# Small matrix products that share the TensorE array: emitted one by one, or as one item per set

## The chip, the cores and the metric

The kernel runs on one NeuronCore of a Trainium2 chip. The metric is the device time of one execution in microseconds (us). The kernel before was timed three times on its own; the median is the number to compare with. All rows below come from one profiled execution of it.

## What is computed

Four transformer blocks on 256 tokens of width 1024, batch 1, in fp32. Each of the ten stages of these blocks is a norm with a shift and scale that come from a conditioning vector, then a mixer or a feed-forward layer, then a gate. Cut to what the change touches:

```python
mod = silu(c) @ ada_w[i] + ada_b[i]            # shift, scale, gate of every stage
h = rms_norm(x, ln) * (1.0 + scale) + shift
x = x + gate * mixer_or_ffn(h)

# mixers: diff_attention, spatial_gating, hgrn2_mixer, nsa_mixer. Of nsa_mixer, for each head:
s_s = q @ k_sel.T * scale - slope * dist        # selected branch
s_w = q @ k_win.T * scale - slope * dist        # window branch
s_c = q @ k_cmp.T * scale - slope * dist_c      # compressed branch, 15 blocks
o = gate0 * softmax(s_c) @ v_cmp + gate1 * softmax(s_s) @ v_sel + gate2 * softmax(s_w) @ v_win
```

At this length all blocks are selected, so the selected branch and the window branch see the same 256 positions, with keys and values of their own.

## The kernel before, in words

**A recorded program.** The methods of `Model` do not emit instructions. Each call on an engine is recorded by `Plan.add` as an `Op` with a priority (its place in the recording), its predecessors and a price from `Plan.price`. `Plan.order` then plays a list scheduler over the five engines: when an engine is free in its model, the ready op of the lowest number goes next, if its tiles find slots (`SLOTS`: 8 PSUM banks `ps`, 4 weight buffers `raw`, 6 `whi`, 6 `wlo`). `Plan.emit` emits all ops in that order (L480), so every instruction carries the line L486, and each engine runs its part strictly in the order planned. Tiles are therefore the way to find a place in the trace.

**The large products.** A weight block arrives by DMA in `raw`; ScalarE writes its high part `whi` and VectorE the remainder `wlo`; TensorE takes three products per pair of tiles (`hhi`·`whi`, `hlo`·`whi`, `hhi`·`wlo`). Up-projections write `pg`, `pv`, `pa`, `pq`, `pc` (256 columns each), down-projections `pd` and the first layer's `pgv` (512 columns).

**The small products.** These are plain fp32 matmuls, which the trace shows as two passes each, and they use part of the 128x128 array:
- `ada` in `first` (L956): shift and scale of the first stage. For each of eight tiles k of the model dimension, 2 x 4 matmuls, each 128 rows by 32 columns of the array, the four of a round in four column strips. Their sums pass through `adas` and `adac` to the columns that scale tile k; beside that the 12 `pgv` products of tile k-1 run. Each k loads 1 MiB of `ada_w` and 0.5 MiB of the feed-forward weights.
- `ada` in `mod_pe` (L706): the same for stage 9, eight sets of four matmuls of 512 columns, worked out beside stage 8.
- `modc` (`mod_cols`, L736) and `modg` (`mod_gate`, L759): sets of four in column strips, beside the feed-forward layers.
- `pl` in `attend` (L1204): logits of the differential attention. Four matmuls per half of the tokens, 64 rows each, two per row strip, recorded map by map.
- `pst` in `recur` (L1403): sets of 16 (or 8, 4) matmuls in column strips of 32 or 64, strip by strip within a block.
- In `nsa_group` (L1637), run for 4 groups of heads and t = 1, 0 (second and first half of the tokens): `npl`, the logits of one head on 64 rows, even heads on rows 0 to 63 and odd heads on rows 64 to 127, one bank each; and `no`, the output of the four heads. `no` has two accumulations in two column strips of 64 (even heads, odd heads), each of one product with the compressed values (`lcT`) and 2 (t = 0) or 4 (t = 1) with the others (`nT`). They are recorded one accumulation after the other:

```python
for e in range(2):
    pairs = [(vc[:, g], lct[0:15, e])]
    pairs += [(vs[br][:, k, es], pts[e][br][:, k]) for br in range(2) for k in range(t + 1)]
    self.mms(o[64 * e:64 * e + 64], pairs)
```

In the model of the kernel before, `price` (L262) gives a matmul of 33 to 64 output rows half of its full time and one of up to 32 a quarter, each by itself; an op of a higher priority number that is ready goes between two ops of such a set whenever the next one of the set is not yet allowed.

Of the kernel before, what the change touches and what calls it, by code (L numbers as in the profile page):

```python
# [54 lines left out]
class Tl:  # L55
    """A tile; those with a tag share the slots of that tag."""
# [57 lines left out]
class Vw:  # L114
    """A view of a tile: how to make it, and which elements it covers."""
# [76 lines left out]
# the scheduler's model: from the end of an instruction to the start of one that waits for it  # L192
# [13 lines left out]
class Plan:  # L206
    ENGINES = ("tensor", "scalar", "vector", "gpsimd", "sync")

    def __init__(self, nc, slots, reserve):
        self.nc, self.slots, self.reserve = nc, slots, reserve  # L210
        self.ops = []
        self.psum = None
        self.shift = 0
        self.turn = None
        self.regret = 2.0
        self.patience = 3000.0
        for e in self.ENGINES:
            setattr(self, e, PlanEngine(self, e))

    def add(self, eng, method, args, kw):  # L220
        op = Op()
        op.eng, op.method, op.args, op.kw = eng, method, args, kw
        op.prio = len(self.ops) + self.shift
        op.succ, op.npred, op.tiles = [], 0, []
# [5 lines left out]
        reads += pos  # L230
# [26 lines left out]
        op.cost, op.late = self.price(op, reads, writes)  # L257
# [4 lines left out]
    def price(self, op, reads, writes):  # L262
        """(what it holds its engine for, what comes on top until its results can be used), in the model"""
        n = max(int(np.prod(v.shape[1:])) for v in (writes[-1:] if op.eng == "tensor" else reads + writes) or reads)
        if op.eng == "sync":
            v = (writes + reads)[0]
            size = int(np.prod(v.shape)) * 4
            return 450.0, size / 360.0
        if op.eng == "tensor":
            if op.method == "transpose":  # L270
                return 109.0, 60.0
            n = int(np.prod(op.args[2].shape[1:]))
            if op.args[2].tl.dtype == F32R:
# [5 lines left out]
        if op.eng == "scalar":  # L279
            aps = sum(isinstance(op.kw.get(x), Vw) for x in ("scale", "bias", "accum_out"))  # L280
            return (51.0 if ps else 94.0) + n * 0.833 + 93.0 * aps, 40.0
        if op.eng == "gpsimd":
            if op.kw.get("op") == OP.pow:
# [3 lines left out]
        if op.method in ("tensor_scalar", "scalar_tensor_tensor"):  # L287
            aps = sum(isinstance(v, Vw) for v in op.args[2:4 if op.method == "tensor_scalar" else 3])
        if op.method in ("tensor_copy", "tensor_scalar", "memset") and not ps:
            return 67.0 + 0.52 * n + 60.0 * aps, 20.0  # L290
        if op.method == "reciprocal":
# [3 lines left out]
    def order(self):  # L295
# [34 lines left out]
        def fits(op):  # L330
            # engines take turns at a bank, for reads too
# [26 lines left out]
        while left:  # L358
            looks.clear()
            for e in self.ENGINES:  # L360
# [22 lines left out]
                if self.regret and e in ("scalar", "vector"):  # L383
                    # a more urgent one that is about to be ready goes first
# [95 lines left out]
    def emit(self):  # L480
# [3 lines left out]
        for op in self.order():  # L484
            f = getattr(getattr(self.nc, op.eng), op.method)
            f(*[real(v) for v in op.args], **{k: real(v) for k, v in op.kw.items()})  # L486
# [7 lines left out]
# the shift and scale (s) and the gate (g) of which stages are worked out beside which stage  # L494
# [6 lines left out]
# how many tiles of a layer's output product wait, to go by half of the tokens  # L501
# [4 lines left out]
class Model:  # L506
# [18 lines left out]
    def m(self, shape, name="m", dtype=F32):  # L525
        """Scratch of the mixers, in the space of the feed-forward activations."""
# [13 lines left out]
    def mms(self, out, pairs):  # L540
        """One accumulation group."""
# [20 lines left out]
    def load(self, t, src):  # L562
        """a weight load: it may run ahead, and the loads after it are issued after it"""
# [14 lines left out]
    def act_pair(self, a32, shape):  # L578
        """Exact high and low parts of an activation, as stationary operands."""
# [7 lines left out]
    def setup(self):  # L587
# [17 lines left out]
        # the first row of each quarter  # L605
# [5 lines left out]
    def columns(self, rows, name):  # L611
        """Vectors cut in rows of 128 -> one column per row."""
# [14 lines left out]
    def load_c(self):  # L627
        """silu of the conditioning vectors, each column 32 times"""
# [5 lines left out]
    def load_columns(self, names, name, maps=(), first=0):  # L634
        """vectors over the model dimension, eight columns each; with them the biases of the stages from `first` on"""
# [9 lines left out]
        if maps:  # L645
            # the 1 that goes with a scale is added here
# [6 lines left out]
    def stage(self, i):  # L653
        """weights, bias, first column, conditioning vector, norm and gate factor of a stage"""
# [25 lines left out]
    def mod_dve(self, i, key):  # L680
        """acc[p, n], with sum over p = (silu(c) @ w)[n] of shift, scale or gate (that with its bias); returns the steps"""
# [24 lines left out]
    def mod_pe(self, i):  # L706
        """shift and scale by matrix products: 512 columns in each quarter of the rows; returns the steps"""
# [3 lines left out]
        def step(k):  # L711
            def f():
# [4 lines left out]
                for j in range(4):  # L717
                    nc.tensor.matmul(self.accc[32 * j:32 * j + 32, :], self.csil[:, coff + k], t[:, j],
                                     start=k == 0, stop=k == 7)
# [8 lines left out]
    def mod_steps(self, item, pe):  # L728
        """Steps that gather the shift and scale, or the gate, of a stage."""
# [6 lines left out]
    def mod_cols(self, i, pe):  # L736
        """Shift and scale of a stage as columns."""
# [3 lines left out]
        else:  # L741
            s = self.pu([128, 512], "modc")
            for j in range(4):
                nc.tensor.matmul(s[32 * j:32 * j + 32, :], self.ones[:, 0:32],
                                 self.acc["sh" if j < 2 else "sc"][:, 512 * (j % 2):512 * (j % 2) + 512],
                                 start=True, stop=True)
# [12 lines left out]
    def mod_gate(self, i):  # L759
        nc = self.nc  # L760
        pt = self.pu([128, 256], "modg")
        for j in range(4):
            nc.tensor.matmul(pt[32 * j:32 * j + 32], self.ones[:, 0:32], self.acc["g"][:, 256 * j:256 * j + 256],
                             start=True, stop=True)
# [6 lines left out]
    def gate_load(self, i):  # L771
        """the gate of a stage, on all partitions"""
# [5 lines left out]
    def rstd(self, ss, parts):  # L778
        """(sum of the first `parts` columns + eps) ** -0.5"""
# [24 lines left out]
    def norm(self, h, r=None, xs=None, x=None):  # L804
        """rms norm with modulation, transposed, as exact high and low parts."""
# [30 lines left out]
    def norm_twice(self, h, row):  # L836
        """x <- rms norm of x times row; then the norm of the next layer."""
# [10 lines left out]
        # with a = mean square + eps: the two norms scale by a ** -.5 and (mean square of x times row / a + eps) ** -.5  # L848
# [13 lines left out]
    def up_t(self, w, c0, new, name):  # L862
        """h @ w[:, c0:c0+256], transposed: [column, 2, token]"""
# [35 lines left out]
    def down_mm(self, h, f, act, parts, cols=(0, 1)):  # L899
        """act = (high, low) parts [128, 256 tokens] of contraction tile f"""  # L900
# [46 lines left out]
    def flip_tokens(self, a):  # L947
        """[token, half, (2, 128)] -> PSUM [128, 2, (half, token)]"""
# [7 lines left out]
    def first(self, wg, wu):  # L956
        """The first norm, and the first 512 columns of the first layer along with it: both go by tiles of the
        model dimension, as the weights of shift and scale come in."""
# [35 lines left out]
        for k in range(9):  # L994
# [17 lines left out]
            for r in range(2):  # L1012
                for j in range(4):
                    nc.tensor.matmul(pa[32 * j:32 * j + 32], self.csil[:, coff + 2 * j + r], t[:, :, 2 * j + r],
                                     start=r == 0, stop=r == 1)
# [3 lines left out]
            for c in range(2):  # L1019
                nc.tensor.matmul(pc[:, c:c + 1], sums[:, c], self.sel, start=True, stop=True)  # L1020
# [95 lines left out]
    def seg_rstd(self, p, nseg, width, name):  # L1116
        """p: [128, nseg, width] -> rstd [128, nseg]"""
# [86 lines left out]
    def attend(self, hp, qt, kt, v):  # L1204
        nc = self.nc
        o_ps = self.pu([128, 2, 2, 128], "o")
        for t in range(2):
            n = 128 * (t + 1)
            # the two maps of both heads; a map's rows of the array write one bank
            lgs = []  # L1210
            sm = self.small(24, "smx")
            for c in range(2):
                cs = slice(64 * c, 64 * c + 64)
                pl = self.pu([128, 2, n], "pl")
                lg = self.m([128, 2, n], "lg")
                for h in range(2):
                    nc.tensor.matmul(pl[:, h], qt[cs, h, 128 * t:128 * t + 128], kt[cs, h, :n],
                                     start=True, stop=True)
# [29 lines left out]
    def to_act(self, on, g):  # L1248
        """[token, (head, half), 128] -> contraction tiles [128, head, token], scaled by column g"""
# [567 lines left out]
```

## Time and profile before

| | us |
|---|---|
| Median of 3 runs | 1757.2 |
| Lowest and highest run | 1753.75, 1757.4 |
| Span of the profiled execution, first to last instruction | 1755.1 |
| TensorE matmuls busy in that span | 1718.1 |
| VectorE busy | 1319.0 |
| ScalarE busy | 953.5 |
| GpSimd busy | 66.3 |

The profile records the span of its execution and not the device time around it; the span lies 2.1 us under the median of the runs, and that is taken as what lies around it. DMA moved 415.00 MB at a mean of 236 GB/s. In the trace a row of TensorE reads: start in us from the span's start, length of the piece in us, operation, output tile and inputs, rows x columns of the array, contraction rows x moving columns, and the number of records (two for each fp32 matmul). Lengths include the time that a result takes to leave the array; how long TensorE is held is the distance to the start of the next piece.

### The profile page before, as it was taken

The page shows a single profiled execution, that of the slowest core. Times are in us where ns is not written, and L with a number is a line of the kernel's source. Part 1 is how long each engine was busy: PE and PEld are TensorE (multiplying, and loading weights), DVE is VectorE, ACT ScalarE, POOL GpSimd, SP SyncE. Part 2 cuts the span into 40 slices and gives each one's busy share as a digit, 9 for nine tenths or more (in the row PEclk, how much of TensorE's full clock was granted, in tenths as well). Part 3 has the DMA queues.
Part 4 walks back from the last instruction along what each step waited for, and adds up shares of the span by engine and source line. Part 5 has one row for each costly group of instructions (what it writes and reads, how often), then busy time and mean ns, then how long its engine had stood idle before and what let it go on. Part 6 is the DMA issues. An engine that isn't in the chain of part 4 may idle for free. (4 is left out here: it accounts for less than half of the span.)

```text
span 1755.1 us, 31103 instructions
## 1 busy us (share of the span) xinstructions
PE 1718.1 (98%) x12678; PEld 1526.4 (87%) x12678; DVE 1319.0 (75%) x2045; ACT 953.5 (54%) x1595; POOL 66.3 (4%) x60
## 2 busy tenths in 40 slices
PE   7999999999999999999999999999999999999998
PEld 4899779899988999798999789979998876579986
DVE  3787679887777878687777788888985556678754
ACT  4454366664446544375444477866553556666542
POOL 0000012100001000000000000000000000000000
PEclk9999999999999999999999999999999999999999
DMA  9798866668886988574889863548887543247662
GB/s 299 266 333 316 284 213 225 206 219 284 294 297 220 344 297 326 180 267 168 294 274 326 328 193 104 199 145 277 290 300 264 191 145 129 82 145 239 201 221 72
DMA packets 264159, 415.00 MB, mean 236 GB/s; under 512 B 12890, under 2 KB 210373, under 8 KB 262993
## 3 DMA queue, kind: packets, MB, share of 16 engines
q1 hardware_dynamic: 264017, 413.03, 69.4%
q8 instruction: 99, 1.62, 0.4%
q14 instruction: 43, 0.35, 0.1%
HBM read 411.90 MB, written 1.10 MB: 235 GB/s over the span
## 5 line engine op out<-in xcount | busy, mean ns | idle before, releaser
L486 ACT ACTIVATE whi<-raw 128x1024 fp32r<-128x1024 f32 x512 | 534.2, 1056 | 516.7 <-PE pd L486 139.9
L486 DVE TENSOR_TENSOR wlo<-raw,whi 128x1024 fp32r<-128x1024 f32 x512 | 616.8, 1220 | 209.1 <-ACT whi L486 207.5
L486 PE MATMUL pv<-hhi,whi 128*128 128x256 f32 x912 | 257.4, 282 | 0.0
L486 PE MATMUL pv<-hhi,wlo 128*128 128x256 f32 x912 | 257.3, 282 | 0.0
L486 PE MATMUL pv<-hlo,whi 128*128 128x256 f32 x912 | 257.1, 282 | 0.0
L486 DVE SCALAR_TENSOR_TENSOR acc<-raw,csil,acc 128x1024 f32<-128x1024 f32 x192 | 245.9, 1281 | 14.4 <-DMA raw<-in_ada_w 11.7
L486 PE MATMUL pd<-whi,ahi 128*128 128x512 f32 x604 | 237.8, 395 | 0.0
L486 PE MATMUL pd<-wlo,ahi 128*128 128x512 f32 x604 | 237.7, 394 | 0.0
L486 PE MATMUL pd<-whi,alo 128*128 128x512 f32 x604 | 237.5, 394 | 0.0
L486 PE MATMUL pg<-hhi,whi 128*128 128x256 f32 x624 | 176.7, 283 | 0.0
L486 PE MATMUL pg<-hlo,whi 128*128 128x256 f32 x624 | 176.2, 282 | 0.0
L486 PE MATMUL pg<-hhi,wlo 128*128 128x256 f32 x624 | 176.0, 282 | 0.0
L486 PEld LDWEIGHTS pv<-hhi,whi 128*128 128x128 f32 x912 | 174.3, 191 | 1.2 <-issue 1.2
L486 PEld LDWEIGHTS pv<-hhi,wlo 128*128 128x128 f32 x912 | 174.4, 191 | 0.0
L486 PEld LDWEIGHTS pv<-hlo,whi 128*128 128x128 f32 x912 | 174.2, 191 | 0.0
L486 PEld LDWEIGHTS pd<-whi,ahi 128*128 128x128 f32 x604 | 113.4, 188 | 30.3 <-issue 5.8
L486 PEld LDWEIGHTS pd<-whi,alo 128*128 128x128 f32 x604 | 113.4, 188 | 25.6 <-issue 0.3
L486 PEld LDWEIGHTS pd<-wlo,ahi 128*128 128x128 f32 x604 | 113.5, 188 | 24.5
L486 PEld LDWEIGHTS pg<-hhi,whi 128*128 128x128 f32 x624 | 119.3, 191 | 2.5 <-issue 2.5
L486 PEld LDWEIGHTS pg<-hlo,whi 128*128 128x128 f32 x624 | 119.3, 191 | 0.1
L486 PEld LDWEIGHTS pg<-hhi,wlo 128*128 128x128 f32 x624 | 119.3, 191 | 0.0
L486 PE MATMUL pa<-hhi,whi 128*128 128x256 f32 x352 | 99.6, 283 | 0.0
(356 smaller groups left out, 3174.3 us busy)
## 6 DMA issues: line engine op xcount, KB each, us to landing
raw<-in_ada_w SPq DMA_DIRECT2D x112, 1024.0 KB
raw<-in_ffn_wd SPq DMA_DIRECT2D x44, 1024.0 KB
raw<-in_ffn_w_up SPq DMA_DIRECT2D x44, 1024.0 KB
raw<-in_ffn_wg SPq DMA_DIRECT2D x42, 1024.0 KB
raw<-in_ffn_wu SPq DMA_DIRECT2D x42, 1024.0 KB
raw<-in_ffn_w_down SPq DMA_DIRECT2D x22, 1024.0 KB
raw<-in_hg_w_in SPq DMA_DIRECT2D x16, 1024.0 KB
raw<-in_attn_w_qkv SPq DMA_DIRECT2D x12, 1024.0 KB
```

The source lines that it names most:

```text
L486: f(*[real(v) for v in op.args], **{k: real(v) for k, v in op.kw.items()})
```

## The change

A context manager `Plan.together` collects matmuls that are recorded inside it into one `Op`, a bundle. The bundle's predecessors are those of all its matmuls together, it becomes ready when all of them could go, holds the engine as one item and is emitted back to back. Its price is 95 ns plus the sum of its matmuls' prices, divided by `pairs`.

```diff
+    @contextmanager
+    def together(self, pairs=1):
+        assert self.bundle is None
+        self.bundle = calls = []
+        yield
+        self.bundle = None
+        self.add("tensor", "bundle", tuple(calls), {}, pairs)
...
+        if method == "bundle":
+            parts = [self.price(eng, m, a, k, *self.operands(a, k)) for m, a, k in args]
+            op.cost, op.late = 95.0 + sum(c for c, _ in parts) / pairs, 60.0
...
     def first(self, wg, wu):
...
+            with nc.together():
+                for r in range(2):
+                    for j in range(4):
+                        nc.tensor.matmul(pa[32 * j:32 * j + 32], self.csil[:, coff + 2 * j + r], t[:, :, 2 * j + r],
+                                         start=r == 0, stop=r == 1)
...
     def attend(self, hp, qt, kt, v):
...
+            with nc.together(2):
+                for h in range(2):
+                    for c in range(2):
...
     def nsa_group(self, g, t, q, vs, vc, gv):
...
+            if j % 2 == 0:
+                pls = [self.pu([128, 2, n], "npl") for e in range(2)]
+                with nc.together(2):
+                    for e in range(2):
+                        rs = slice(64 * e, 64 * e + 64)
+                        nc.tensor.matmul(pls[e], q[rs, j // 2, ts], kt[rs, :, :n], start=True, stop=True)
+            pl = pls[j % 2]
...
-        for e in range(2):
-            pairs = [(vc[:, g], lct[0:15, e])]
-            pairs += [(vs[br][:, k, es], pts[e][br][:, k]) for br in range(2) for k in range(t + 1)]
-            self.mms(o[64 * e:64 * e + 64], pairs)
+        with nc.together():
+            for i in range(len(terms[0])):
+                for e in range(2):
+                    nc.tensor.matmul(o[64 * e:64 * e + 64], *terms[e][i], start=i == 0, stop=i == len(terms[0]) - 1)
```

`mod_pe`, `mod_cols`, `mod_gate` and `recur` get a `together` around their sets as `first` does. In `attend` the rows of the two maps take turns; in `nsa_group` an even and an odd head share a bundle of `npl`, and the two strips of `no` take turns. The arithmetic is the same, instruction for instruction. The planner's other rules are as they were; since prices and sets differ, the order of all engines differs in places, ScalarE's 27 table loads keep their number.

On TensorE in `first`, around one k of the loop, the kernel before has:

```order
L486 MATMUL ada<-raw,csil 32x256 x5
L486 MATMUL pgv<-whi,hhi 128x512
L486 MATMUL ada<-raw,csil 32x256
L486 MATMUL pgv<-wlo,hhi 128x512
L486 MATMUL ada<-raw,csil 32x256
L486 MATMUL pgv<-whi,hlo 128x512
L486 MATMUL ada<-raw,csil 32x256
L486 MATMUL pgv<-whi,hhi 128x512
```

and the changed kernel:

```order
L511 MATMUL pgv<-whi,hlo 128x512
L511 MATMUL ada<-raw,csil 32x256 x8
L511 MATMUL pgv<-whi,hhi 128x512
L511 MATMUL pgv<-wlo,hhi 128x512
L511 MATMUL pgv<-whi,hlo 128x512
```

The last three of the eight `ada` stood alone between `pgv` products at four of the eight k (k = 2 to 5; the other four sets were whole already); now all eight sets are whole. In the same way `mod_pe`'s eight sets of four, four of which stood in two groups, are now whole. The sets `modc`, `modg` and all 28 small sets of `pst` stood back to back before, in the same order.

On TensorE in `nsa_group`, t = 0, around one `no` (buffer numbers kept; the two `nT` are those of even and of odd heads), the kernel before has:

```order
L486 MATMUL npl_16363<-kt_15146,q_15300 128x256
L486 MATMUL npT_16370<-ident_82,lg_16315 128x128
L486 MATMUL npl_16372<-kt_15146,q_15300 128x256
L486 MATMUL npT_16370<-ident_82,lg_16315 128x128
L486 MATMUL pd_16150<-whi_16022,nact_16074 128x512
L486 MATMUL no_16384<-lcT_16368,vc_15817 64x256
L486 MATMUL no_16384<-nT_16247,v_15038 64x256
L486 MATMUL no_16384<-nT_16247,v_15066 64x256
L486 MATMUL no_16384<-lcT_16368,vc_15817 64x256
L486 MATMUL no_16384<-nT_16291,v_15038 64x256
L486 MATMUL no_16384<-nT_16291,v_15066 64x256
```

and the changed kernel:

```order
L511 MATMUL npl_16371<-kt_15146,q_15301 128x256
L511 MATMUL npl_16373<-kt_15146,q_15301 128x256
L511 MATMUL pd_16085<-wlo_16087,nact_16064 128x512
L511 MATMUL no_16386<-lcT_16368,vc_15864 64x256 x2
L511 MATMUL no_16386<-nT_16284,v_15038 64x256
L511 MATMUL no_16386<-nT_16293,v_15038 64x256
L511 MATMUL no_16386<-nT_16284,v_15066 64x256
L511 MATMUL no_16386<-nT_16293,v_15066 64x256
L511 MATMUL npl_16406<-kt_15146,q_15301 128x256
L511 MATMUL npl_16408<-kt_15146,q_15301 128x256
```

Of the 32 `npl`, 20 stood alone (4 of t = 1, all 16 of t = 0); now all stand in pairs of an even and an odd head. The eight `no` sets stood whole, but strip after strip; now the strips take turns. The number of instructions on each engine is the same.

## Rows read from the trace of the kernel before

**Rows 1.** Page, busy us (share of the span) and instructions of each engine.
```profile
PE 1718.1 (98%) x12678; PEld 1526.4 (87%) x12678; DVE 1319.0 (75%) x2045; ACT 953.5 (54%) x1595; POOL 66.3 (4%) x60
```
**Rows 2.** Windows by stage: length, busy us by engine, granted clock, DMA share, GB/s.
```profile
0.00:60.00 60.00, 50.65 (x270) 30.22 (x271) 24.90 (x67) 24.89 (x51) 2.71 (x9) 1.00 1.01 296
...
1020.00:1160.00 140.00, 138.14 (x1795) 127.31 (x1795) 117.35 (x217) 114.27 (x231) 6.97 (x6) 1.00 0.48 155
...
1405.00:1488.00 83.00, 81.14 (x498) 58.90 (x496) 49.64 (x179) 48.52 (x118) 0.00 (x0) 0.94 0.41 141
1488.00:1550.00 62.00, 60.98 (x277) 34.96 (x277) 44.44 (x225) 38.31 (x136) 1.50 (x2) 1.00 0.19 63
```
**Rows 3.** Timeline of PE, the loop of `first`.
```profile
42.70 1.05 PE L486 MATMUL ada<-raw,csil 128*32 128x256 f32 x10
43.68 0.50 PE L486 MATMUL pgv<-whi,hhi 128*128 128x512 f32 x1
44.11 0.62 PE L486 MATMUL ada<-raw,csil 128*32 128x256 f32 x2
44.66 0.51 PE L486 MATMUL pgv<-wlo,hhi 128*128 128x512 f32 x1
...
46.96 0.40 PE L486 MATMUL pgv<-wlo,hhi 128*128 128x512 f32 x1
47.19 0.39 PE L486 MATMUL pgv<-whi,hlo 128*128 128x512 f32 x1
...
49.34 1.07 PE L486 MATMUL ada<-raw,csil 128*32 128x256 f32 x16
50.34 0.50 PE L486 MATMUL pgv<-whi,hhi 128*128 128x512 f32 x1
...
53.99 1.07 PE L486 MATMUL ada<-raw,csil 128*32 128x256 f32 x16
```
**Rows 4.** Timeline of PE, two `no` sets: t = 1, then t = 0.
```profile
1457.31 0.64 PE L486 MATMUL no<-lcT,vc 15*64 15x256 f32 x2
...
1459.75 0.64 PE L486 MATMUL no<-lcT,vc 15*64 15x256 f32 x2
...
1462.19 0.39 PE L486 MATMUL pq<-hhi,whi 128*128 128x256 f32 x1
...
1513.24 0.64 PE L486 MATMUL no<-lcT,vc 15*64 15x256 f32 x2
...
1514.82 0.64 PE L486 MATMUL no<-lcT,vc 15*64 15x256 f32 x2
```
**Rows 5.** Timeline of PE, `npl`: t = 1 alone, t = 1 paired, t = 0 alone.
```profile
1464.07 1.12 PE L486 MATMUL npl<-kt,q 64*128 64x512 f32 x2
...
1465.66 1.13 PE L486 MATMUL npl<-kt,q 64*128 64x512 f32 x4
...
1506.88 0.70 PE L486 MATMUL npl<-kt,q 64*128 64x256 f32 x2
1507.51 0.50 PE L486 MATMUL pd<-whi,nact 128*128 128x512 f32 x1
```
**Rows 6.** Timeline of PE, `ada` of stage 9: a whole set, then one in two groups.
```profile
1396.09 1.06 PE L486 MATMUL ada<-raw,csil 128*32 128x512 f32 x8
...
1415.59 1.05 PE L486 MATMUL ada<-raw,csil 128*32 128x512 f32 x4
...
1416.94 1.05 PE L486 MATMUL ada<-raw,csil 128*32 128x512 f32 x4
```
**Rows 7.** Timeline of PE, one pair of `pl` sets of the differential attention.
```profile
257.57 1.68 PE L486 MATMUL pl<-qT 64*128 64x128 f32 x16
```
**Rows 8.** Waits of PE: us in total, times, longest.
```profile
PE ph L486 <- issue: 1.9, 1, 1.9
```
**Rows 9.** Windows, 10 us behind that wait.
```profile
1440.00:1450.00 10.00, 10.00 (x54) 7.89 (x53) 4.91 (x35) 4.23 (x16) 0.00 (x0) 0.53 0.44 145
```
**Rows 10.** Timeline of PE in that window, three of a set's four `ada`.
```profile
1445.46 1.93 PE L486 MATMUL ada<-raw,csil 128*32 128x512 f32 x6
```

More of the change, by code (lines that the diff above doesn't have):

```diff
@@ L1 @@
 import math
-from contextlib import ExitStack
+from contextlib import ExitStack, contextmanager
 import numpy as np
@@ L229, in add @@
             writes.append(pos.pop(0))
-        reads += pos
+        return reads + pos, writes
+    def add(self, eng, method, args, kw, pairs=1):
+        if self.bundle is not None:
+            assert eng == "tensor"
+            self.bundle.append((method, args, kw))
+            return None
+        op = Op()
+        op.eng, op.method, op.args, op.kw = eng, method, args, kw
+        op.prio = len(self.ops) + self.shift
+        op.succ, op.npred, op.tiles = [], 0, []
+        calls = [self.operands(a, k) for _, a, k in args] if method == "bundle" else [self.operands(args, kw)]
+        reads, writes = [v for r, _ in calls for v in r], [v for _, w in calls for v in w]
         preds = set()
@@ L286, in price @@
         aps = 0
-        if op.method in ("tensor_scalar", "scalar_tensor_tensor"):
-            aps = sum(isinstance(v, Vw) for v in op.args[2:4 if op.method == "tensor_scalar" else 3])
-        if op.method in ("tensor_copy", "tensor_scalar", "memset") and not ps:
+        if method in ("tensor_scalar", "scalar_tensor_tensor"):
+            aps = sum(isinstance(v, Vw) for v in args[2:4 if method == "tensor_scalar" else 3])
+        if method in ("tensor_copy", "tensor_scalar", "memset") and not ps:
             return 67.0 + 0.52 * n + 60.0 * aps, 20.0
-        if op.method == "reciprocal":
+        if method == "reciprocal":
             return 65.0 + 6.2 * n, 20.0
@@ L716, in f @@
                 self.load(t, w[128 * k:128 * k + 128, off:off + 2 * D].rearrange("p (j f) -> p j f", j=4))
-                for j in range(4):
-                    nc.tensor.matmul(self.accc[32 * j:32 * j + 32, :], self.csil[:, coff + k], t[:, j],
-                                     start=k == 0, stop=k == 7)
+                with nc.together():
+                    for j in range(4):
+                        nc.tensor.matmul(self.accc[32 * j:32 * j + 32, :], self.csil[:, coff + k], t[:, j],
+                                         start=k == 0, stop=k == 7)
                 if k == 7:
@@ L742, in mod_cols @@
             s = self.pu([128, 512], "modc")
[L743 to L746, printed above, removed]
+            with nc.together():
+                for j in range(4):
+                    nc.tensor.matmul(s[32 * j:32 * j + 32, :], self.ones[:, 0:32],
+                                     self.acc["sh" if j < 2 else "sc"][:, 512 * (j % 2):512 * (j % 2) + 512],
+                                     start=True, stop=True)
             r = self.P.tile([128, 512], F32, name="sums", tag="sums")
@@ L761, in mod_gate @@
         pt = self.pu([128, 256], "modg")
-        for j in range(4):
-            nc.tensor.matmul(pt[32 * j:32 * j + 32], self.ones[:, 0:32], self.acc["g"][:, 256 * j:256 * j + 256],
-                             start=True, stop=True)
+        with nc.together():
+            for j in range(4):
+                nc.tensor.matmul(pt[32 * j:32 * j + 32], self.ones[:, 0:32], self.acc["g"][:, 256 * j:256 * j + 256],
+                                 start=True, stop=True)
         row = self.P.tile([128, 256], F32, name="grow", tag="sums")
@@ L1011, in first @@
             pa = self.pu([128, 2, 128], "ada")
[L1012 to L1015, printed above, removed]
+            with nc.together():
+                for r in range(2):
+                    for j in range(4):
+                        nc.tensor.matmul(pa[32 * j:32 * j + 32], self.csil[:, coff + 2 * j + r], t[:, :, 2 * j + r],
+                                         start=r == 0, stop=r == 1)
             sums = self.s([128, 2, 128], "adas")
@@ L1018, in first @@
             pc = self.pu([128, 2], "adac")
-            for c in range(2):
-                nc.tensor.matmul(pc[:, c:c + 1], sums[:, c], self.sel, start=True, stop=True)
+            with nc.together():
+                for c in range(2):
+                    nc.tensor.matmul(pc[:, c:c + 1], sums[:, c], self.sel, start=True, stop=True)
             b = self.bcol[0]
@@ L1411, in blocks @@
             p = self.pu([128, 4, 32], "pst")
-            for i in range(4):
-                for j in range(4):
-                    sl = slice(128 * i + 32 * j, 128 * i + 32 * j + 32)
-                    nc.tensor.matmul(p[32 * j:32 * j + 32, i], l[:, sl], r[:, sl], start=True, stop=True)
+            with nc.together():
+                for i in range(4):
+                    for j in range(4):
+                        sl = slice(128 * i + 32 * j, 128 * i + 32 * j + 32)
+                        nc.tensor.matmul(p[32 * j:32 * j + 32, i], l[:, sl], r[:, sl], start=True, stop=True)
             return p
@@ L1434, in recur @@
                 p = self.pu([128, 4, m], "pst")
-                for i in range(4):
-                    for s0 in range(0, 128, 2 * m):
-                        nc.tensor.matmul(p[s0:s0 + m, i], x[:, 128 * i + s0:128 * i + s0 + m],
-                                         x[:, 128 * i + s0 + m:128 * i + s0 + 2 * m], start=True, stop=True)
+                with nc.together():
+                    for i in range(4):
+                        for s0 in range(0, 128, 2 * m):
+                            nc.tensor.matmul(p[s0:s0 + m, i], x[:, 128 * i + s0:128 * i + s0 + m],
+                                             x[:, 128 * i + s0 + m:128 * i + s0 + 2 * m], start=True, stop=True)
                 for s0 in range(0, 128, 2 * m):
@@ L1655, in nsa_group @@
         for j in range(4):
-            rs = slice(64 * (j % 2), 64 * (j % 2) + 64)
-            pl = self.pu([128, 2, n], "npl")
-            nc.tensor.matmul(pl, q[rs, j // 2, ts], kt[rs, :, :n], start=True, stop=True)
+            if j % 2 == 0:
[5 more added lines that the diff above has]
+            pl = pls[j % 2]
             lg = self.m([128, 2, n], "lg")
```

52 lines of the change are left out of this document (28 added, 24 removed).

## The prediction

> **What bounds the kernel now.** I read the page first. TensorE is busy 1718.1 of 1755.1 us [rows 1]; its idle time is 37.0 us in all, so a microsecond that its instructions no longer hold it is worth up to a microsecond at the end, unless another engine or the DMA is close behind. Who is close behind has to be read stage by stage, in the windows [rows 2]: in the loop of `first` it is the DMA (share 1.01, 296 GB/s), in stage 8 (1405 to 1550) VectorE, with 49.64 of 83 us and 44.44 of 62 us, while the DMA has room (0.41, 0.19). Then I read the timeline around each of the small sets, since a busy TensorE says nothing of how well the array is filled: distances between starts tell that.
>
> In [rows 3] a whole set of eight `ada` (16 records) holds TensorE from 49.34 to 50.34, 1.00 us. One `ada` alone holds it from 44.11 to 44.66, 0.55 us. Eight of them one after the other could not fit into 1.00 us at that price: the four column strips work at the same time. And a `pgv` that stands between two lone `ada` takes 0.43 us (43.68 to 44.11) instead of 0.23 (46.96 to 47.19), so each trip from the full array to a strip and back costs 0.20 us beside the product itself. Those are the two prices that the change plays on.
>
> **The change, part by part.**
>
> *Loop of `first`.* A period with a split set is 6.64 us (42.70 to 49.34) and holds 12 `pgv`; the period with a whole set is 4.65 us (49.34 to 53.99) and holds, by the order, 13 of them, so 4.65 - 0.23 = 4.42 us for the same work [rows 3]. Four periods lose 2.22 us each: **8.9 us**. What is late next is the DMA. Up to the last tile of the loop it has to bring x (1 MiB) and 7 x 1.5 + 1 MiB, 13.1 MB; at 296 GB/s [rows 2] that takes 44.3 us. TensorE wants that tile at 53.99 now and at 45.1 then. It just fits; if the first transfers start late, 1 or 2 us go. The two ends are 4 and 8.9; I take 8, near the upper one, because the sum above says that the data is there.
>
> *`no`.* One strip holds TensorE 2.44 us at t = 1 (1457.31 to 1459.75), and the second strip another 2.44 (to 1462.19); at t = 0 one strip takes 1.58 (1513.24 to 1514.82) [rows 4]. If two strips of 64 columns overlap as the four of 32 do in [rows 3], each set costs one strip's time: 4 x 2.44 + 4 x 1.58 = **16.1 us**. The trace has no set of two column strips that take turns, so the ends are 0 (they do not overlap) and 16.1. I take the upper: strips of the same 128 rows, in one bank, with accumulation over two rounds, are what `ada` has too.
>
> A rule speaks against this term. The Trainium skill, "TensorE: Matmul & The Clock Gate", Part 3, says that a weight load overlaps a running matmul only where the row group differs; the strips of `no` and of `ada` share all rows. By that rule the term would be near 0 and the whole sum about 16 us smaller. The 1.00 us of a whole `ada` set [rows 3] speaks for the overlap, and I follow the row.
>
> *`npl`.* At t = 1 one alone has length 1.12 us and a pair of both row strips 1.13 [rows 5]: the second is free. Four stand alone there, they become two pairs: 2 x 1.05 = 2.1 us (start distances are 0.07 shorter than these lengths). At t = 0 one alone holds TensorE 0.63 us (1506.88 to 1507.51), and 16 become 8 pairs: 8 x (0.63 + 0.20 for the trip) = 6.6 us. Together **8.7 us**.
>
> *`ada` of stage 9.* Half a set is as long as a whole one, 1.05 against 1.06 us [rows 6]. Four sets stand in two groups: 4 x 1.0 = **4.0 us**.
>
> *`pl`.* Eight matmuls last 1.68 us [rows 7], and there are four such pieces, 6.7 us in all. Serial passes would be gained back at most by half, 3.4 us; but a lone pass of 256 moving columns in the rows of `npl` takes about 0.3 us (0.63 for two), so the 16 passes here would take over 3 us if they did not overlap already. I take 0. *`pst`, `modc`, `modg`* were back to back in the same strips: 0, hidden by nothing, because nothing moves.
>
> *What is added.* No instruction. A bundle must wait for all of its inputs: `no` for both halves of its heads, `npl` for two free banks. What queues behind it on TensorE are `pd`, `pq` and transposes, which the planner can put ahead. VectorE and ScalarE get the logits of two heads at once. Elsewhere the order shifts by a few places (transposes of the next norm, positions of `abp`); I bound that by 2 us either way and take 0.
>
> *The clock.* Behind a 1.9 us wait [rows 8] the granted clock was 0.53 over 10 us [rows 9], the lower of the two levels, 1.2 instead of 2.4 GHz, for most of it. Three `ada` took 1.93 us there [rows 10] where a whole set takes 1.06 [rows 6]. Such a stretch costs between 0.9 us (this piece alone) and 5.1 us (half of 10.2 us). The order around it is now another; it may vanish or move. I take 1.5 us gained, half of a middle price of 3.
>
> **What cannot be kept.** Stage 8 would lose 16.1 + 8.7 + 4.0 = 28.8 of 145 us. VectorE has 94.1 us of work there, 81% of what is left. In the recurrence stage TensorE is busy 138.14 of 140 us beside a VectorE that is busy 117.35, 84% [rows 2], so that density alone can be borne. But the second part, 1488 to 1550, holds four t = 0 and one t = 1 `no`, 16 `npl` and two split `ada`: 4 x 1.58 + 2.44 + 6.6 + 2 = 17.4 us would leave 44.6 us for VectorE's 44.44. At 84 to 90% it needs 49 to 53 us. Some of that work moves ahead, so I take off 6 us: 28.8 - 6 = 23 us.
>
> **Sum.** 8 + 23 + 1.5 = 32.5 us off the span of 1755.1, which gives 1722.6; with the 2.1 us by which the median of the runs lies above it, **1724 us**.
>
> **The rivals.**
> - *VectorE's chains take over stage 8.* From the logits on, each group goes through VectorE, ScalarE, VectorE, TensorE, VectorE and back; with less `pq` and `pd` to cover it TensorE waits. For it: the 44.44 us above. Against it: 1405 to 1488 has a VectorE busy only 60%. If half of the 28.8 us is lost: 8 + 14 - 1 = 21 us, 1736 us.
> - *Column strips of the same rows do not overlap in `no`.* 37.7 - 16.1 = 21.6 us of work saved, less 2 for the loop and the rest: about 19 us, 1738 us. Against it: [rows 3].
> - *The DMA holds the loop of `first`.* Then that term is 4 instead of 8: 1728 us.
> - *Slower: the clock stays low in stage 8.* TensorE's work there becomes thinner, with waits between; if each leads to a stretch like [rows 9] at up to 5.1 us, 7 of them undo the sum, and eleven (the whole stage) cost 56 us: 1780 us. Against it: between 1488 and 1550, with the smallest products, the clock was 1.00 [rows 2], and only the one wait of 1.9 us was followed by a fall.
> - *Nothing comes of it:* the shifted order in other stages costs what is gained. I see no stage that moves by that much: 1757 us.
>
> **How the numbers follow.** Forecast 0.60; VectorE's chains 0.21; strips 0.06; DMA 0.07; low clock 0.03; nothing 0.03. The best case is 37.7 + 5.1 us, 1714; the weak cases reach 1738, and both together some us more, so the range is 1714 to 1741. About 0.2% (3.5 us) is what a measurement of this kernel can tell from no change: faster 0.94, same 0.03, slower 0.03.
>
> **What would show each step.** Right: the period of the loop of `first` is near 4.4 us at every k; a `no` set is 2.4 to 2.6 us at t = 1 and 1.6 at t = 0; pairs of `npl` at t = 0 take 0.63 us; TensorE's busy time falls by over 25 us and stage 8 is some 23 us shorter. Wrong: `no` still takes 4.88 us, or stage 8 shows idle time of TensorE of 10 us and more before `npT`, `no` or `pd`, or the windows show a granted clock of 0.5 in several places there, or the loop waits for `raw`.

## The result, and the profile after

The changed kernel takes **1727.6 us** (median of 4 runs, 1726.84 to 1727.91) where the kernel before takes 1755.8 beside it (1753.75 to 1757.4; the three runs of the table before and a fourth): ratio 0.9835, 95% interval 0.9822 to 0.9849, 28.2 us faster. The span of the profiled execution went from 1755.1 to 1725.1 us, 30.0 us less. The first line of the page of the changed kernel, which answers to [rows 1]:

```profile
PE 1684.6 (98%) x12678; PEld 1515.7 (88%) x12678; DVE 1317.4 (76%) x2045; ACT 953.3 (55%) x1595; POOL 64.3 (4%) x60
```

TensorE is busy 33.5 us less with as many instructions, and its idle time rose from 37.0 to 40.5 us. Where the 30.0 us came from is read by cutting both executions at the same work: the last transpose of each norm, `xT`. Windows of the kernel before (length, busy time of PE, PEld, DVE, ACT, POOL, granted clock, DMA share, GB/s): stage 0, the differential attention, the feed-forward layer behind it, the recurrence, the layer behind that, and stage 8.

```profile
12.70:239.20 226.50, 224.90 (x1496) 189.89 (x1495) 160.68 (x203) 100.76 (x143) 3.93 (x4) 1.00 0.88 291
239.20:364.70 125.50, 120.71 (x893) 108.47 (x892) 108.72 (x233) 82.49 (x174) 26.12 (x14) 1.00 0.61 208
364.70:559.20 194.50, 192.71 (x1372) 178.48 (x1370) 145.36 (x160) 95.17 (x130) 5.88 (x6) 1.00 0.79 272
...
1029.70:1178.70 149.00, 144.41 (x1810) 131.97 (x1808) 124.98 (x225) 116.53 (x235) 7.29 (x6) 0.99 0.50 162
1178.70:1373.30 194.60, 194.55 (x1392) 179.86 (x1390) 156.58 (x190) 106.74 (x149) 2.90 (x3) 1.00 0.77 263
1373.30:1562.80 189.50, 185.49 (x1108) 132.38 (x1106) 121.09 (x443) 113.63 (x297) 2.90 (x3) 0.97 0.41 136
```

The same six of the changed kernel:

```profile
12.50:232.90 220.40, 216.34 (x1483) 187.97 (x1481) 159.95 (x202) 101.41 (x143) 3.92 (x4) 1.00 0.90 298
232.90:360.40 127.50, 121.17 (x886) 109.65 (x885) 110.75 (x235) 82.61 (x176) 25.20 (x14) 0.97 0.65 217
360.40:556.60 196.20, 195.00 (x1393) 180.76 (x1391) 143.50 (x158) 94.69 (x130) 5.87 (x6) 1.00 0.76 263
...
1027.00:1172.90 145.90, 141.69 (x1796) 129.03 (x1795) 122.88 (x223) 116.23 (x233) 6.38 (x6) 1.00 0.50 164
1172.90:1369.20 196.30, 196.25 (x1404) 181.35 (x1403) 158.11 (x192) 107.22 (x150) 2.90 (x3) 1.00 0.77 261
1369.20:1533.40 164.20, 159.65 (x1112) 121.97 (x1110) 121.52 (x444) 113.31 (x296) 2.87 (x3) 0.98 0.49 163
```

The lengths differ by 6.1, -2.0, -1.7, 3.1, -1.7 and **25.3** us; the stages left out give 0.9 together. Stage 8 is nearly the whole of it: TensorE loses 25.8 us of work there and waits half a microsecond more, while VectorE does the same 121 us in 164 instead of 190.

The transposes themselves moved a little in the order, so neighbouring stages trade a microsecond or two in these differences. The sets `modg`, which stand in both kernels once in most stages, are steadier marks. They start at 222.82, 400.67, 934.79, 1216.22, 1348.30 and 1702.28 us before and at 218.21, 397.87, 932.16, 1211.92, 1344.13 and 1672.22 us after: 4.6, 2.8, 2.6, 4.3, 4.2 and 30.1 us ahead. So 4.6 us are gained by the end of stage 0, 1.8 are lost in the differential attention and 0.2 behind it, 1.7 come back in the recurrence, and 25.9 are gained between the marks around stage 8.

The pieces themselves, in the timeline of TensorE of the changed kernel (start, length, operation, rows x columns, contraction rows x moving columns, records): two sets of `ada` in `first`, one of stage 9, a `no` set at t = 1 and one at t = 0, and a pair of `npl` at t = 0.

```profile
37.32 1.07 PE L511 MATMUL ada<-raw,csil 128*32 128x256 f32 x16
38.32 0.50 PE L511 MATMUL pgv<-whi,hhi 128*128 128x512 f32 x1
...
41.74 1.07 PE L511 MATMUL ada<-raw,csil 128*32 128x256 f32 x16
...
1430.15 1.07 PE L511 MATMUL ada<-raw,csil 128*32 128x512 f32 x8
1431.15 0.38 PE L511 MATMUL pq<-hhi,whi 128*128 128x256 f32 x1
...
1461.52 0.65 PE L511 MATMUL no<-lcT,vc 15*64 15x256 f32 x4
1462.10 1.95 PE L511 MATMUL no<-nT,v 128*64 128x256 f32 x16
1463.97 0.38 PE L511 MATMUL pq<-hhi,whi 128*128 128x256 f32 x1
...
1487.29 0.65 PE L511 MATMUL no<-lcT,vc 15*64 15x256 f32 x4
...
1488.89 0.70 PE L511 MATMUL npl<-kt,q 64*128 64x256 f32 x4
1489.52 0.28 PE L511 MATMUL pTc<-ident,lc 128*15 128x128 f32 x1
```

The period of the loop of `first` is 4.42 us (37.32 to 41.74). A whole `no` set is 2.45 us at t = 1 (1461.52 to 1463.97) where [rows 4] has 4.88, and 1.60 at t = 0 (1487.29 to 1488.89) where [rows 4] has 3.16: twice the records in the time of one strip. A pair of `npl` takes 0.63 us (1488.89 to 1489.52), as one alone did [rows 5].

### The profile page after: what moved, and what is told of

Same layout as the page of the kernel before. It is cut to its first block, busy times and chain, and to the rows that moved or that the text cites. A ratio compares the mean times of both kernels' runs of the same rounds, so it can differ in the third digit from the quotient of the medians.

```text
span 1725.1 us, 31089 instructions
## 1 busy us (share of the span) xinstructions
PE 1684.6 (98%) x12678; PEld 1515.7 (88%) x12678; DVE 1317.4 (76%) x2045; ACT 953.3 (55%) x1595; POOL 64.3 (4%) x60
## 5 line engine op out<-in xcount | busy, mean ns | idle before, releaser
L511 DVE SCALAR_TENSOR_TENSOR acc<-raw,csil,acc 128x1024 f32<-128x1024 f32 x192 | 246.0, 1281 | 15.3 <-DMA raw<-in_ada_w 13.0
```

Source lines behind the costliest of these rows:

```text
L511: f(*[real(v) for v in args], **{k: real(v) for k, v in kw.items()})
```

## Experiments

Three theories. **Overlap**: sets in different strips run at the same time once they stand together, and the gain is the sum of the sets' prices. **Order**: an item of its own with a better price gives the planner a better order, and the strips add little. **VectorE**: its chains take over stage 8 and hold most of the gain back. Ratios are to the kernel before beside the same runs.

| Run | median us | ratio, 95% interval |
|---|---|---|
| `serial_no` | 1738.3 | 0.9907, 0.9882 to 0.9932 |
| `no_alone` | 1738.6 | 0.9903, 0.9879 to 0.9926 |
| `npl_alone` | 1746.1 | 0.9946, 0.9928 to 0.9964 |
| `first_alone` | 1751.9 | 0.9977, 0.9964 to 0.9990 |
| `ada9_alone` | 1749.2 | 0.9957, 0.9941 to 0.9972 |
| `rest_alone` | 1758.4 | 1.0012, 0.9997 to 1.0026 |
| `without_rest` | 1726.8 | 0.9833, 0.9818 to 0.9849 |
| `cols_late` | 1726.4 | 0.9824, 0.9807 to 0.9841 |
| `rows_own` | 1730.6 | 0.9861, 0.9840 to 0.9881 |
| `ph_strips` | 1721.1 | 0.9800, 0.9780 to 0.9819 |
| `after_again` | 1725.4 | 0.9820, 0.9801 to 0.9839 |
| `ph_fewer` | 1721.5 | 0.9792, 0.9772 to 0.9813 |

**The same plan, strip after strip.** In `serial_no` every engine has the planned order of the changed kernel, instruction for instruction; inside the eight bundles of `no` alone the matmuls are sorted by strip again.

```diff
+SERIAL = ("no",)
...
-            for i in range(len(terms[0])):
-                for e in range(2):
+            order = [(i, e) for i in range(len(terms[0])) for e in range(2)]
+            if "no" not in SETS or "no" in SERIAL:
+                order.sort(key=lambda v: v[1])
+            if True:
+                for i, e in order:
```

> The changed kernel with every bundle and the same planned order on every engine; inside the eight `no` bundles alone the strips go one after the other, as in the kernel before. Overlap theory (two strips of 64 columns that take turns work at the same time): a `no` set takes 4.88 us at t = 1 and 3.16 at t = 0 again instead of 2.45 and 1.60; 4 x 2.43 + 4 x 1.56 = 16.0 us more on TensorE, of which a few may hide in its waits of some 4 us in that stage: 1739 to 1744 us. Order theory (the bundles give the planner a better order, the strips add little): 1728 to 1731 us.

1738.3 us, 10.8 more than the changed kernel, 13.0 more than its second measurement below; by the ratios, which set each run against the kernel before beside it, 12.6 and 15.3 us. Its timeline has a t = 1 set at the old 4.89 us (1464.08 to 1468.97):

```profile
1464.08 0.64 PE L514 MATMUL no<-lcT,vc 15*64 15x256 f32 x2
...
1466.52 0.64 PE L514 MATMUL no<-lcT,vc 15*64 15x256 f32 x2
...
1468.97 0.38 PE L514 MATMUL pq<-hhi,whi 128*128 128x256 f32 x1
```

Since nothing but the turns of the strips differs, those turns are worth the difference. For `no` the order theory falls. (Both executions have a stretch of low clock near the end of the stage, 0.84 from 1498 to 1520 us in both, so the clock does not make the difference.) Against the changed kernel the same instructions start 2.0 us earlier ahead of the first set and 11.7 us later behind the last, so the stage is 13.7 us longer; of the 16.0 us on TensorE some 2.3 are hidden. Half of that is seen: TensorE's waits of `pd` for `nact` at the end of the stage (ScalarE's and VectorE's work) are 1.7 us in the changed kernel and 0.5 here. The total lies just under the range expected.

**Each part alone.** These are the kernel before with one kind of set bundled (`first` with the pairs `adac` behind its `ada`); the others are recorded as before.

```diff
-    def together(self, pairs=1):
+    def together(self, pairs=1, of=""):
...
+        if of not in SETS:
+            yield
+            return
...
+SETS = ("no",)
```

> The kernel before, with the bundle of `no` alone, strips taking turns. Overlap theory: 16 us off stage 8, clock stretches aside (3 us either way): 1737 to 1744 us where the kernel before has 1756. VectorE theory (its chains take over once TensorE is faster there): under 10 us, 1747 or more. Order theory: 1753 to 1758.

1738.6 us, 16.6 less than the kernel before, in the overlap theory's range and far from VectorE's.

> The kernel before, with the bundles of `npl` alone. By the prices in the prediction 20 lone `npl` become 10 pairs, 2.1 + 6.6 = 8.7 us: 1745 to 1750 us where the kernel before has 1756. If logits of two heads at once only move the work of VectorE (VectorE theory): 1753 or more.

1746.1 us, 9.2 less, as the overlap theory has it.

> The kernel before, with the bundles of `first` alone. Overlap theory: the loop is 7.6 us shorter as in the changed kernel; then TensorE meets the small loads behind the loop early and waits for them in three places, 3.0 us, so 4.6 us stay: 1750 to 1753 us where the kernel before has 1756. If the loads of the loop set its end: under 2 us gained, 1754 to 1757.

1751.9 us, 3.3 less (its profiled span 5.2 less). On the same instructions the gain is 7.9 us between 40 and 60 us and 4.2 from 80 us on, with the three waits for small loads in between (1.3, 0.8 and 0.4 us). That is the expected shape; but in this execution, which had its full pace from 19.3 us on (the changed kernel from 23.7), the DMA was already at its edge. Its timeline shows `ada` waiting for its load at three k:

```profile
31.45 1.07 PE L514 MATMUL ada<-raw,csil 128*32 128x256 f32 x16 [0.36 <-DMA raw<-in_ada_w]
36.40 1.07 PE L514 MATMUL ada<-raw,csil 128*32 128x256 f32 x16 [0.45 <-DMA raw<-in_ada_w]
41.33 1.07 PE L514 MATMUL ada<-raw,csil 128*32 128x256 f32 x16 [0.44 <-DMA raw<-in_ada_w]
```

> The kernel before, with the bundles of stage 9's `ada` (mod_pe) alone. Overlap theory: four split sets become whole, 4 x 1.0 us, and up to 2.5 us more if the stretch of low clock behind the wait of `ph` goes, as it did with `no` or `npl` alone: 1749 to 1753 us where the kernel before has 1755. Rival, the split halves were hidden in other waits: 1754 to 1757.

1749.2 us, 7.1 less: in range, and more than the 4.0 us of the sets. The stretch of low clock of [rows 9] is missing in this execution, and in those of `no_alone` and `npl_alone` too. In the stage the three gained 8.7, 18.2 and 11.8 us on the same instructions, where their sets are worth 4.0, 16.0 and 8.7: that leaves 4.7, 2.2 and 3.1 us for the stretch and for whatever else the new order brings. In `first_alone` and `rest_alone`, which do not touch the order there, it stood at the same place.

> The kernel before, with the bundles that the prediction costs at nothing alone: `pl` (rows of the two maps in turn), `pst`, `modc`, `modg`. Overlap theory: no set becomes faster; the shifted order of the differential attention may cost up to 2 us: 1754 to 1758 us where the kernel before has 1755. Rival, the planner's better price for them gives a better order: under 1752.

1758.4 us, 2.1 more, with an interval that holds no change and up to 2.6 parts in 1000. Taken together these four bundles gain nothing. In the trace they do move time: by the `modg` marks this execution falls from 1.2 us ahead of the kernel before (at 222 us) to 2.1 behind (at 401), and is 1.4 behind at 1216.

> The changed kernel without those four bundles; `first`, stage 9's `ada`, `npl` and `no` remain. Overlap theory: all of the gain is in these, so as the changed kernel or up to 2 us faster: 1724 to 1728 us. Rival, the other bundles contribute: 1731 or more.

1726.8 us, as the changed kernel. All of its gain is in `first`, stage 9's `ada`, `npl` and `no`. The medians of the four alone add up to 36.2 us; if three of them include the stretch of low clock of the kernel before, at the mean of 3.3 us that the traces left for it, it can go but once: an estimate of 36.2 - 6.6 = 29.6, against the 28.2 and 31.9 us measured for all together.

**What gives back a part of the loop's gain.** On the same instructions the changed kernel is 7.6 us ahead behind the loop of `first` and 4.6 us ahead from 72 us on. Its waits of TensorE between 50 and 100 us:

```profile
PE cols L511 <- DMA rows<-in_attn_k_norm: 1.0, 1, 1.0
PE cols L511 <- DMA rows<-in_ffn_conv_w: 0.6, 1, 0.6
PE cols L511 <- DMA rows<-in_ada_b: 0.6, 1, 0.6
```

The kernel before has none there. `cols` are the transposes of small vectors, whose loads stand between the large ones in SyncE's queue. Two attempts to get this back; the first records the transposes later, the second gives the landing tiles more room, so that they do not wait for one another.

```diff
+        nc.shift = self.late
         nc.tensor.transpose(pt, st, self.ident[:total, :total])
...
+        self.late = 150
```

> The changed kernel with the transposes `cols` behind the loop of `first` recorded 150 places later, so that they do not meet their small loads (and with them some of these loads go later, since their buffers come free later). If the 3.0 us that the loop's gain gives back are these three waits: 1724 to 1726 us. Rival, the large loads of the first layer hold it anyway: 1727 to 1728.

```diff
-        st = self.s([total, 128], "rows")
+        st = self.m([total, 128], "rows")
```

> The changed kernel, with the landing tiles `rows` of the small loads in the space of the mixers' scratch (22 slots) instead of 2 shared slots, so that these loads no longer wait for one another in SyncE's queue. If this queue is what gives back 3.0 of the 7.6 us of the loop of `first`: up to 3 us faster, 1724.5 to 1726.5. Rival, the loads of 1 MiB hold the work behind the loop whatever the order: 1727 to 1729.

`cols_late` measured 1726.4, between both expectations, and its execution still waits 1.8 us for two of these loads: it decides nothing. `rows_own` measured 1730.6, slower than either theory said. All small loads now go ahead of the large ones, and the wait has changed its owner, a wait for the first feed-forward weights:

```profile
PE pg L511 <- ACT whi L511: 4.2, 1, 4.2
```

Behind that wait its clock is low for a stretch (0.89 from 40 to 72 us, where the changed kernel has 1.00), worth up to 3.5 us by an estimate from the window (32 us at 0.89), so the run does not price the queue's order alone.

So 2.2 of the 3.0 us are seen as waits for small loads, and moving these loads only moved the wait. That another order of the queue would win it back is not shown: between 40 and 72 us the DMA's share is 0.89 (284 GB/s) where it was 0.71 (227), and a DMA that is nearly full there would do the same. No run separates the two.

**A further set.** `ph` in `nsa_hidden` (the hidden layer of the compression) is one sum of 16 products in one strip of 64 columns. Its even and odd terms can go to two strips.

```diff
-        ph = self.pu([64, 5, 15], "ph")
+        ph = self.pu([128, 5, 15], "ph")
...
+        with nc.together():
+            for l in range(16):
+                e, t = l % 2, 2 * l
+                nc.tensor.matmul(ph[64 * e:64 * e + 64], cw1[:, l], kcv[:, :, t // 16:t // 16 + 15, t % 16],
+                                 start=l < 2, stop=l > 13)
+        hs = self.s([64, 5, 15], "phs")
+        nc.scalar.activation(hs, ph[64:128], AF.Copy)
+        nc.vector.tensor_tensor(hs, ph[0:64], hs, op=OP.add)
```

> The changed kernel, and `ph` of stage 8 goes into two column strips too: its 16 products, one sum in one strip of 64 columns until now, take turns between two strips, and a copy and an addition of [64, 75] put the two sums together. In the changed kernel such a set holds TensorE 4.25 us. Overlap theory: 2.15 us each, two sets, 4.2 us off, less what the longer chain behind them costs (two small operations, some 0.5 us): 1722 to 1725 us where the changed kernel has 1727.6. Rival, VectorE's chains already set the end of stage 8: 1726 to 1729.

1721.1 us (1718.23 to 1722.29), a little better than expected: 6.5 us under the changed kernel's first measurement and 4.3 under its second, 6.1 and 3.5 by the ratios. The set in the changed kernel, then in this one, each with what follows it:

```profile
1414.43 4.32 PE L511 MATMUL ph<-raw,cw 128*64 128x75 f32 x32
1418.68 0.39 PE L511 MATMUL pq<-hlo,whi 128*128 128x256 f32 x1
```

```profile
1414.26 2.34 PE L511 MATMUL ph<-raw,cw 128*64 128x75 f32 x32
1416.53 0.39 PE L511 MATMUL pc<-hhi,wlo 128*128 128x256 f32 x1
```

4.25 us became 2.27. The stage's second set, which a piece of `pcs` divides in the changed kernel, went from 4.38 to 2.27: 4.1 us together. The execution shown gained 7.4 us in the stage; it has no stretch of low clock at its end, and the changed kernel's has one, so more than the sets is in that number.

**The clock.** Two last runs side by side: the changed kernel once more, and `ph` in strips without the four bundles that gain nothing in total.

> The changed kernel as it is, once more, on the same chip as the run beside it: 1726 to 1729 us. If the stretches of low clock belong to the planned order, its trace shows them at 245, 355 and 1501 us again and nowhere else; if an execution may or may not have one behind the same wait, at least one of them is gone or another is there.

> The changed kernel with `ph` in two strips and without the four bundles `pl`, `pst`, `modc`, `modg`. If the order of the differential attention with the bundles of `pl` costs what stages 1 and 2 lost in the changed kernel: 2 to 3 us faster than with `ph` alone, 1718 to 1720 us. If that loss is only where the clock happened to fall: 1720 to 1723.

`after_again` measured 1725.4 us (1722.2 to 1726.95). The window from 1500 to 1510 us of the first execution of the changed kernel, then of this one:

```profile
1500.00:1510.00 10.00, 9.39 (x35) 5.27 (x36) 7.26 (x43) 5.29 (x23) 0.00 (x0) 0.66 0.32 105
```

```profile
1500.00:1510.00 10.00, 8.68 (x49) 5.32 (x47) 9.63 (x57) 7.65 (x30) 0.09 (x1) 1.00 0.33 106
```

The waits around it are the same in both executions, to the tenth of a microsecond (`npT` for VectorE's `lg` 1.0 us in two pieces, `no` for `lcT` 0.2 us), and the order is the same. One had the lower clock, the other not, and on the same instructions that is 2.8 us (from 1.06 behind to 1.72 ahead). The stretches at 245 and 355 us were in both. So the same wait on TensorE can be followed by a fall or not.

The other stretches go with the plan far more closely. At the end of stage 1 and at the end of the recurrence, the kernel before, then the changed kernel:

```profile
354.00:359.00 5.00, 4.43 (x32) 3.88 (x31) 3.95 (x8) 4.77 (x12) 0.00 (x0) 1.00 0.00 0
1170.00:1175.00 5.00, 4.31 (x23) 3.94 (x24) 4.68 (x10) 5.00 (x14) 0.00 (x0) 0.66 0.08 17
```

```profile
354.00:359.00 5.00, 4.22 (x24) 3.98 (x23) 4.55 (x10) 3.71 (x11) 0.87 (x1) 0.66 0.31 92
1170.00:1175.00 5.00, 3.93 (x34) 3.73 (x33) 4.43 (x10) 4.65 (x11) 0.87 (x1) 1.00 0.64 213
```

In the kernel before `xT` waits 2.9 us in one piece for VectorE's `xs`, up to 1170.56 us, and the clock falls; in the changed kernel that wait is 2.3 us in two pieces, and the clock holds. At the end of stage 1 it is the other way about: there the changed kernel's `xT` waits 2.6 us for `xs`, up to 353.23 us. All seven traces without the bundles of `pl`, `pst`, `modc` and `modg` have the stretch at the end of the recurrence (at 1166 to 1173 us) and none at the end of stage 1. Of the seven with them, six have the one in stage 1 (at 352 to 360 us) and not the other; `cols_late` is the exception, with the wait of 2.6 us, no fall behind it, and the stretch at 1169.

`ph_fewer` measured 1721.5 us (1716.99 to 1722.3), by the ratios 1.4 us faster than `ph_strips`, which the intervals (some 3.5 us either way) cannot tell from none or from 3. Its trace says more than its median. Against `after_again` it gains 3.7 us in stage 1 (from 0.74 us behind at the `modg` of 218 us to 2.97 ahead at 398), where it has no stretch of low clock and `after_again` has two, and it has given 2.7 of them back by the `modg` of 1213 us, partly in the recurrence, at whose end it has one. So the plan with the four bundles does cost time in stage 1, and wins most of it back later. The two stretches alone are worth up to 3.4 us, an estimate from the windows (5 us at 0.66 lose 1.7 us each); how much of the loss is theirs and how much the order's own is not separated.

## Why the prediction was right, and where its steps were off

The forecast of 1724 us lies 3.6 us under the median, the range of 1714 to 1741 holds it, and the mechanism is the one predicted: 32.5 us off the span were forecast, 30.0 came. (The sum of the prediction is a little off: 1722.6 + 2.1 is 1724.7 and not 1724.)

- **Loop of `first`, 8 us: right in the loop, too high for what stays.** The period is 4.42 us at k = 2 to 5, as worked out, and the loop ends 7.6 us sooner. The missing 1.3 of 8.9 were lost ahead of k = 2, where TensorE ran at half its pace for longer (`pgv` 0.43 us apart until 23.4 us, before until 20.2). The step "what is late next is the DMA" was looked for in the large loads and answered too soon: behind the loop TensorE waits for small loads, 2.2 us of the 3.0 given back there, and 4.6 us stayed. The rival of the DMA (a term of 4) is right in size for this term, by another transfer.
- **`no`, 16.1 us: right.** 4.88 to 2.45 and 3.16 to 1.60 is 4 x 2.43 + 4 x 1.56 = 16.0 us of TensorE. In the changed kernel's order 13.7 us of that reach the end of the stage.
- The rule against it did not hold here. By that one rule of the Trainium skill, "TensorE: Matmul & The Clock Gate", Part 3, taken alone, this term would have been near 0; the prediction passed over the table of the same Part, which gives 2.38 times the speed for three tiles of 32 columns. Another page of the Trainium skill, "TensorEngine Tiling (Array Packing)", section "Tiling Modes", says that different tiles of the array can load weights and multiply in parallel, two tiles for 64 columns. The 2.45 us for two strips beside 2.44 for one agree with the second rule and speak against the first.
- **`npl`, 8.7 us: right.** 9.2 us alone, 3 of them perhaps the clock's; a pair takes 0.63 us at t = 0 and 1.06 at t = 1.
- **`ada` of stage 9, 4.0 us: right.** Each set is 1.00 us long.
- **`pl`, `pst`, `modc`, `modg`, 0: right in total.** `rest_alone`, `without_rest` and `ph_fewer` show no clear difference. That nothing moves is wrong: by the `modg` marks stage 1 is 2.7 to 3.7 us longer with these bundles in all four pairs of traces that can be set side by side (`rest_alone` with the kernel before, the changed kernel with `without_rest`, `after_again` and `ph_strips` with `ph_fewer`); by 1217 us the first pair has 0.7 us of it back, the others most or all.
- **The discount of 6 us: too large by some 2 us.** The stage lost 25.3 of 28.8 us, clock included. VectorE is busy 74% of the stage (121.5 of 164.2 us) and holds TensorE little: its waits there come to 4.6 us, 4.0 before. That VectorE's chains took the 3.5 us is not shown; `serial_no` hides 2.3 us, half of it at waits for `nact`.
- **The clock, 1.5 us gained: wrong as a gain.** The stretch of [rows 9] went, and with it one at 1171 us that the prediction had not looked for; others came at 245, 355 and 1501 us. The mean granted clock of the whole execution is 0.995 before and after. The price was about right: 2.8 us between two executions of one kernel, and 2.2 to 4.7 us left over for the one of the kernel before, in the bounds of 0.9 to 5.1.
- **The order elsewhere, 0, bounded by 2 us: right, at its bound.** By the `modg` marks 2.0 us are lost in stages 1 and 2 and 1.7 come back in the recurrence. The clock's stretches there, two new ones in stage 1 and one that is gone at the end of the recurrence, are worth up to 1.7 us each by the estimate above; the prediction did not count them, and they are enough to make both numbers.

On the same instructions the sum closes so: 4.6 us from the loop instead of 8, about 0.4 lost between there and stage 8 instead of 0, and 25.9 in stage 8, clock included, instead of 23 and 1.5. That the total comes within 4 us of the forecast is in part luck, since the loop came out too high and the discount took off too much.

## What to carry to other kernels

Look at small matmuls by the distance between starts, not by the busy share: a TensorE that is 98% busy held some 30 us of time in sets that used a half or a quarter of the array one after the other or broke up the work around them. Sets in different strips have to be emitted back to back and in turns; a scheduler that prices each by itself will slip other work between them or leave a strip's accumulation in one piece. And where a stage with a margin gets faster, ask for the small loads behind it as well as for the large ones.

## What was not expected of the hardware

- Two strips of 64 columns over the same 128 rows, each with a sum of 5 terms, cost no more than one (2.45 us beside 2.44). The 16 terms of `ph` in two strips take 2.27 us instead of 4.25, a little over half.
- The same instructions in the same order, behind the same waits, ran at the lower clock in one execution and not in the next (0.66 beside 1.00 in the window above).
- At the very start the granted clock of the records does not tell the pace. The changed kernel's window from 17.5 us reads 1.00:

```profile
17.50:23.50 6.00, 6.00 (x23) 4.46 (x16) 3.91 (x9) 2.56 (x6) 0.00 (x0) 1.00 1.15 312
```

  and yet plain `pgv` products start 0.43 us apart in it, and 0.23 behind it:

```profile
20.80 0.63 PE L511 MATMUL pgv<-wlo,hhi 128*128 128x512 f32 x1
21.23 0.63 PE L511 MATMUL pgv<-whi,hlo 128*128 128x512 f32 x1
21.66 0.63 PE L511 MATMUL pgv<-whi,hhi 128*128 128x512 f32 x1
...
25.36 0.40 PE L511 MATMUL pgv<-wlo,hhi 128*128 128x512 f32 x1
25.59 0.40 PE L511 MATMUL pgv<-whi,hlo 128*128 128x512 f32 x1
25.83 0.40 PE L511 MATMUL pgv<-whi,hhi 128*128 128x512 f32 x1
```
